# Two transformer blocks in one program: when the MLP writes the second block's split weight slabs to DRAM

## The chip, the cores and the metric

One core of a Trainium2 chip runs the whole program. Its engines are TensorE (PE, with its weight loads PEld), VectorE (DVE), ScalarE (ACT), GpSimd (POOL) and SyncE (SP), which issues nearly all DMAs. The metric is the device time of one execution in microseconds (us).

## The reference

The input `x` is 512 tokens by 1024 channels, float32. Two blocks follow each other:

```
# first block
h = rmsnorm(x, ln1);  z = h @ w_in
mix = [pooling means, chunked gated linear attention (decay, state), forgetting attention]
x = x + mix @ w_o
h = rmsnorm(x, ln2);  gate, up = split(h @ w_gu);  x = x + (silu(gate) * up) @ w_down   # MLP, 2816 wide
x = rmsnorm(x, ln_f)
# second block
h = rmsnorm(x, g);  q_lat, c_kv, k_rope, z_a, q_b, k_b, v_b, z_b, q_idx, k_idx, w_idx, gate_a, gate_b = split(h @ w_in)
y_a = latent attention(q_lat, c_kv, k_rope) * silu(z_a)
y_b = attention over the 128 keys chosen by the indexer (q_idx, k_idx, w_idx), plus a bias by distance, * silu(z_b)
merged = sigmoid(gate_a) * (y_a @ w_o_a) + sigmoid(gate_b) * (y_b @ w_o_b)
out = rmsnorm(x + merged @ w_out)
```

## The kernel before

**Products.** Channels lie on the partitions, tokens on the free axis. Every large product is made of float32 numbers split in two: a high part (`hi`, rounded by ACT's copy into the type fp32r) and a low part (`lo = src - hi`). One product of 128 by 128 by 512 is three matmuls, hi·hi, hi·lo, lo·hi (`dense`, L200). A weight slab (128 x 1024, 512 KB) is loaded into `wr`, ACT writes `wh`, and DVE or POOL writes `wl` (`weight`, L194; `split`, L186). There are two buffers of `wr` and three each of `wh` and `wl`.

**Order of the work.** TensorE's instructions run in the order in which the code writes them. The order on ACT, DVE, POOL and SP is chosen by the framework's scheduler when the program is built, from dependences, priorities and its own estimate of durations. Each of these engines then runs its list strictly in order and waits at the first instruction that is not ready. `issue_after(x)` orders the instructions of its block that run on the engine of `x` behind `x`; `high_priority` lets them go first.

**The first norm** (`block1`, L496): the squares of `x` are added on DVE into `ss`; PE sums them over channels (`tr<-ones,ss`), DVE makes `part` from the result, and PE spreads it over all partitions (`tr<-identr,part`), which ACT copies as `R`. The decay product of the gated linear attention (`tr<-ga,c_wau`, in `decay`) waits for `R`; the transposes `tr<-c_ident,b` need what is computed from it.

**The MLP** (`mlp`, L854) runs in two halves. A half has 11 gate/up iterations (two slabs of `w1gu` each, 48 matmuls), whose last step splits the result into `fh` (ACT) and `fl` (DVE); then eight down products (`down`, 33 matmuls each). A down product's weight of 704 KB is loaded into `wd` and split into `wdh` (ACT) and `wdl` (DVE); each of these has two buffers. Before the first iteration `entry` (L833) multiplies three slabs ahead of the second norm and spreads that norm's factor as `R`.

**Slabs split ahead.** During the MLP the kernel also prepares 27 slabs of the second block (`store`, L241): load into `sr` (two buffers), split into `sh` (ACT) and `sl` (POOL), one buffer each, and write both to DRAM (`h_w2s<-sh`, `l_w2s<-sl`, and the like for `w2pair`, `w2uq_r`). The second block then reads the two parts straight into `wh` and `wl` (`ready`, L231). The queue `ahead` (L884) holds these slabs; one is taken at the start of every gate/up iteration but the first, and one behind every second down product. Nothing but the buffers ties a `store` to that place.

**The bias by distance** (`relative`, L979, at the start of the second block): two small products make a table of 8 x 640 (`gd` in DRAM), and one DMA inside DRAM copies it 128 times per head into `shear` (2560 KB), from which each head of the last attention reads a skewed window.

Of the kernel before, what the change touches and what calls it, by code (L numbers as in the profile page):

```python
# [11 lines left out]
F32 = mybir.dt.float32  # L12
# [3 lines left out]
AF = mybir.ActivationFunctionType  # L16
# [68 lines left out]
class Body:  # L85
# [100 lines left out]
    def split(self, hi, lo, src, eng=None):  # L186

        self.nc.scalar.activation(hi, src, AF.Copy)  # L188
        (eng or self.nc.vector).tensor_tensor(lo, src, hi.bitcast(F32), op=OP.subtract)  # L189
# [37 lines left out]

    def slab(self, name, i, n=1024):
        return lambda: self.ready(name, i, n)
# [11 lines left out]
    def store(self, pool, name, i, n=1024):  # L241

        nc = self.nc
        raw = pool.tile([P, 1024], F32, tag="sr", name="sr", bufs=2)[:, :n]
        nc.sync.dma_start(raw, self.A[name][i])
        hi, lo = (pool.tile([P, 1024], F32R, tag=t, name=t, bufs=1)[:, :n] for t in ("sh", "sl"))
        self.split(hi, lo, raw, nc.gpsimd)
        self.stored[name, i] = kept = []
        for part, src in (("h", hi), ("l", lo)):
            kept.append(self.dp.tile([P, n], F32, name=f"{part}_{name}_{i}"))  # L250
            nc.sync.dma_start(kept[-1], src.bitcast(F32))
# [35 lines left out]
    def parts(self, c):  # L287

        n = c.shape[1]
        hi, lo = (self.gp.tile([P, 8], F32R, tag="part", name="part", bufs=6)[:, :n] for _ in "hl")  # L290
        self.nc.vector.tensor_copy(hi, c)
        self.nc.vector.tensor_tensor(lo, c, hi.bitcast(F32), op=OP.subtract)
        return hi, lo

    def spread(self, parts):

        ps = self.bank("tr")
        for t in range(NT):
            for a, c in enumerate(parts):
                self.mm(ps[:, t * P:(t + 1) * P], c[:, t:t + 1].to_broadcast([P, P]), self.identr, a == 0, a == 1)  # L300
        r = self.row()
        self.nc.scalar.activation(r, ps, AF.Copy)
        return r
# [9 lines left out]
    def square_into(self, ssum, src, first, scale=1.0, eng=None):  # L313
        nc = self.nc
        if first:
            nc.scalar.activation(ssum, src, AF.Square, scale=scale)
        else:
            sq = self.tmp()
            nc.scalar.activation(sq, src, AF.Square, scale=scale)  # L319
            (eng or nc.gpsimd).tensor_tensor(ssum, ssum, sq, op=OP.add)  # L320
# [175 lines left out]
    def block1(self, ctx, raw):  # L496
# [25 lines left out]
        for k in range(KD):  # L522
            with self.tc.issue_after(getattr(last, "ins", last)):
                self.square_into(ssum, x[k], k == 0, eng=nc.vector)
# [18 lines left out]
        next(gen)  # L543
        next(gen)
        R, Rc = self.all(r)
        psk = self.all(gen)
# [27 lines left out]
    def gla_phase(self, ctx, h, R, Rc, mix, mp, b, fd, psg, held, V, proj):  # L574
# [24 lines left out]
        def gates():  # L599
# [3 lines left out]
            nc.vector.tensor_tensor(z, psg[:64], t, op=OP.add)  # L603
# [9 lines left out]
        def gla_v():  # L613
            yield from self.take()
            w = [self.weight(A["w1gv"][a]) for a in range(2)]
# [7 lines left out]
        def qk(f, held=None):  # L623
            q, k = gx(), gx()
            ps = held[0] if held else (yield from self.dense(self.slab("w1s", T1["gq"] + f), h))
# [113 lines left out]
        def chain(f, held=None):  # L739
# [3 lines left out]
            yield QKW  # L743
# [109 lines left out]

    def mlp(self, ctx):  # L854
# [17 lines left out]
        def turn(m):  # L872
# [5 lines left out]
            for t in range(NT):  # L878
# [5 lines left out]
        t2 = lambda name, n: [("w2s", T2[name] + i, 1024) for i in range(n)]  # L884
        ahead = deque([("w2m", 0, KD * 72)] + t2("c_kv", 2) + t2("q_idx", 2) + t2("q_lat", 3) + [("w2kv_v", 0, 1024)]
                      + t2("gate_b", 8) + [("w2uq_r", 0, 768), ("w2pair", 0, 640)] + t2("gate_a", 2) + t2("z_a", 1)
                      + [("w2pair", 1, 640)] + t2("gate_a", 4)[2:] + t2("z_a", 2)[1:] + [("w2pair", 2, 640)])
        turns = []
        for half in range(2):
            for k in range(FH):  # L890
                m = half * FH + k
                if m and ahead:
                    self.store(wd, *ahead.popleft())
# [11 lines left out]
                self.split(act[k][0], act[k][1], u)  # L905
            for m in range(KD):
                ps = self.all(self.dense(down(m, half), act, kt=FH))
                if m % 2 and ahead:
                    self.store(wd, *ahead.popleft())
                nc.vector.tensor_tensor(x[m], ps, x[m], op=OP.add)  # L910
# [39 lines left out]
    def block2(self, ctx, psm, psc):  # L950
# [11 lines left out]
        relb = self.const(bp, "relb", [32, 8])  # L962
        wc = bp.tile([P, NT, 8], F32, name="wc")
        shear = self.dp.tile([8, P * 641], F32, name="shear")
# [13 lines left out]

        def relative():  # L979

            onehot = at("ph", 2, (P, 1024))[:32, :640]
            nc.sync.dma_start(onehot, A["onehot"])
            gd = self.dp.tile([8, 640], F32, name="gd")
            g8 = at("pl", 2, (P, 1024))[:8, :640]
            yield 9000
            for c in range(0, 640, 320):
                ps = self.bank("tr")
                self.mm(ps[:8, :320], relb, onehot[:, c:c + 320])
                nc.scalar.activation(g8[:, c:c + 320], ps[:8, :320], AF.Copy, scale=-1.0)
            nc.sync.dma_start(gd, g8)  # L990

            dst = bass.AP(tensor=shear.tensor, offset=shear.offset, ap=[[P * 641, 8], [641, P], [1, 640]])
            nc.sync.dma_start(dst, bass.AP(tensor=gd.tensor, offset=gd.offset, ap=[[640, 8], [0, P], [1, 640]]))
# [214 lines left out]
        self.spawn(relative())  # L1208
# [300 lines left out]
```

## Time and profile before

| | |
|---|---|
| median of 3 runs | 1075.25 us (1071.88 to 1076.89) |
| the profiled execution | 1080.48 us, of which the span from the first to the last instruction is 1078.7 us |
| PE busy | 1049.3 us, 97% of the span, 5264 matmuls |
| DVE, ACT, POOL busy | 654.2, 544.8, 368.5 us (61%, 51%, 34%) |
| mean granted clock of TensorE | 0.989 |
| DMA | 167.68 MB; slices 10 to 16 of 40 carry 257 to 355 GB/s, most others 57 to 230 |

The profile is one execution. A row of a timeline gives an instruction's start, its length, and in brackets the idle time of its engine just before it and what ended that idle time. A row of a window gives the busy time of each engine in a stretch, with the number of instructions, then TensorE's granted clock (1.00 is 2.4 GHz, 0.50 is 1.2 GHz), the share of time in which the DMA engines were busy, and GB/s. The matmul's length in the profile includes its pipeline; the pace is seen from starts.

### The profile page before, as it was taken

The numbers are of one execution on the slowest core, as the hardware profiler recorded it, in microseconds if no ns is written. First come the engines' busy times: TensorE is split into PE (matmuls) and PEld (weight loads), VectorE is DVE, ScalarE is ACT, GpSimd is POOL, SyncE is SP. The second block draws the span as 40 slices with busy tenths as digits, with TensorE's granted clock in tenths as the row PEclk, the third lists the DMA queues.
The fourth block names the chain that finished last, engine by engine and source line by source line (L and its number), as shares of the span: only waits on it lengthen the run. The fifth ranks groups of instructions, "written<-read, shape, count | busy, mean of one in ns | idle before, by whom it ended". The sixth has DMA issues, their size and how long they took to land.

```text
span 1078.7 us, 14278 instructions
## 1 busy us (share of the span) xinstructions
PE 1049.3 (97%) x5264; PEld 867.9 (80%) x5264; DVE 654.2 (61%) x1140; ACT 544.8 (51%) x954; POOL 368.5 (34%) x214
## 2 busy tenths in 40 slices
PE   8999999999999998999999999999999999999997
PEld 5888877787888776888888887888887898888786
DVE  6653488876656432345433335699995566887652
ACT  6763578746443432233314545545565556777233
POOL 2233322144555533223212310010024336655354
PEclk9999999999999998999999999999999999999999
DMA  6312222129898879432343146464532323335742
GB/s 224 104 59 79 62 104 64 67 80 355 288 320 302 287 257 310 163 111 83 107 141 100 57 147 226 165 216 163 177 125 81 117 78 118 110 99 166 282 145 79
DMA packets 57246, 167.68 MB, mean 155 GB/s; under 512 B 6680, under 2 KB 11176, under 8 KB 57176
## 3 DMA queue, kind: packets, MB, share of 16 engines
q1 hardware_dynamic: 54088, 160.45, 44.3%
q10 hardware_dynamic: 2448, 4.22, 1.0%
q0 software_dynamic: 640, 2.10, 0.5%
q8 instruction: 42, 0.69, 0.3%
q14 instruction: 28, 0.23, 0.1%
HBM read 129.81 MB, written 39.56 MB: 157 GB/s over the span
## 4 chain that ended last, share of the span: by engine, by line
PE 70%; DMA 12%; DVE 10%; ACT 4%; POOL 2%; issue 1%; SPq 1%; ACTq 0%; POOLq 0%; DVEq 0%
PE mm L151 57%; DMA h_w2s<-sh 6%; PE sc L151 5%; PE pv L151 3%; PE tr L158 2%; PE tr L151 2%; DMA l_w2s<-sl 2%; DMA wl<-l_w2s 1%; POOL sl L189 1%; ACT sh L188 1%; DMA h_w2pair<-sh 1%; DVE pl L409 1%; DVE b L333 1%; DVE score L1046 1%; DVE b L396 1%
## 5 line engine op out<-in xcount | busy, mean ns | idle before, releaser
L151 PE MATMUL mm<-hh,wh 128*128 128x512 f32 (+2 forms) x808 | 324.9, 402 | 4.8 <-ACT hh L516 1.9
L151 PE MATMUL mm<-hl,wh 128*128 128x512 f32 (+3 forms) x808 | 316.4, 392 | 0.6 <-DVE hl L517 0.6
L151 PE MATMUL mm<-hh,wl 128*128 128x512 f32 (+1 forms) x800 | 313.3, 392 | 1.1 <-DMA wl<-l_w2s 0.6
L189 POOL TENSOR_TENSOR wl<-wr,wh 128x1024 fp32r<-128x1024 f32 x80 | 198.9, 2487 | 332.5 <-ACT wh L188 311.2
L188 ACT ACTIVATE wh<-wr 128x1024 fp32r<-128x1024 f32 (+2 forms) x115 | 119.6, 1041 | 137.2 <-PE mm L151 107.0
L151 PEld LDWEIGHTS mm<-hh,wh 128*128 128x128 f32 (+1 forms) x808 | 153.1, 189 | 36.5 <-ACT hh L516 2.7
L151 PEld LDWEIGHTS mm<-hh,wl 128*128 128x128 f32 (+1 forms) x800 | 150.7, 188 | 34.7 <-DMA wl<-l_w2s 0.9
L151 PEld LDWEIGHTS mm<-hl,wh 128*128 128x128 f32 (+2 forms) x808 | 152.6, 189 | 29.0 <-DVE hl L517 1.9
L189 POOL TENSOR_TENSOR sl<-sr,sh 128x1024 fp32r<-128x1024 f32 (+3 forms) x27 | 66.6, 2466 | 77.3 <-DMA l_w2s<-sl 48.1
L151 PE MATMUL mm<-fh,wdh 128*128 128x512 f32 x176 | 71.8, 408 | 5.8 <-ACT fh L188 3.7
L151 PE MATMUL mm<-fh,wdl 128*128 128x512 f32 x176 | 71.5, 406 | 1.0 <-DVE wdl L189 0.9
L188 ACT ACTIVATE sh<-sr 128x1024 fp32r<-128x1024 f32 (+3 forms) x27 | 27.0, 1000 | 88.7 <-DMA h_w2s<-sh 46.0
L151 PE MATMUL mm<-fl,wdh 128*128 128x512 f32 x176 | 71.2, 404 | 0.4 <-DVE fl L189 0.4
L189 DVE TENSOR_TENSOR wl<-wr,wh 128x1024 fp32r<-128x1024 f32 (+1 forms) x34 | 51.7, 1522 | 25.4 <-ACT wh L188 24.1
L320 POOL TENSOR_TENSOR ss<-ss,t 128x512 f32<-128x512 f32 x21 | 30.2, 1446 | 101.1 <-ACT t L319 90.0
L189 DVE TENSOR_TENSOR fl<-u,fh 128x512 fp32r<-128x512 f32 x22 | 39.9, 1813 | 28.3 <-ACT fh L188 28.3
L409 DVE TENSOR_TENSOR pl<-tr,ph 128x128 fp32r<-128x128 f32 (+1 forms) x96 | 46.0, 483 | 11.2 <-ACT ph L408 10.1
L393 ACT ACTIVATE s<-s,m 128x128 f32<-128x128 f32 (+1 forms) x64 | 35.8, 560 | 31.8 <-DVE m L391 31.6
L151 PE MATMUL mm<-wh,hh 128*128 128x256 f32 x160 | 46.5, 290 | 0.0
L151 PEld LDWEIGHTS mm<-fh,wdh 128*128 128x128 f32 x176 | 34.1, 194 | 14.5 <-ACT fh L188 4.2
L910 DVE TENSOR_TENSOR x<-mm,x 128x512 f32<-128x512 f32 x16 | 11.0, 690 | 57.0 <-PE mm L151 57.0
L408 ACT ACTIVATE ph<-tr 128x128 fp32r<-128x128 f32 (+1 forms) x96 | 40.4, 426 | 9.9 <-PE tr L158 9.4
(343 smaller groups left out, 2038.8 us busy)
## 6 DMA issues: line engine op xcount, KB each, us to landing
wr<-in_w1gu SPq DMA_DIRECT2D x44, 512.0 KB, 4.4
wd<-in_w1d SPq DMA_DIRECT2D x16, 704.0 KB, 4.9
sr<-in_w2s SPq DMA_DIRECT2D x21, 512.0 KB, 5.6
h_w2s<-sh SPq DMA_DIRECT2D x21, 512.0 KB, 6.5
l_w2s<-sl SPq DMA_DIRECT2D x21, 512.0 KB, 3.9
wh<-h_w2s SPq DMA_DIRECT2D x21, 512.0 KB, 3.7
wl<-l_w2s SPq DMA_DIRECT2D x21, 512.0 KB, 4.6
wr<-in_w2s SPq DMA_DIRECT2D x18, 512.0 KB, 3.5
```

What stands on the lines that cost most here:

```text
L151: self.nc.tensor.matmul(out, l, r, start=start, stop=stop)
L158: self.nc.tensor.transpose(out, src, self.ident if ident is None else ident)
L188: self.nc.scalar.activation(hi, src, AF.Copy)
L189: (eng or self.nc.vector).tensor_tensor(lo, src, hi.bitcast(F32), op=OP.subtract)
L320: (eng or nc.gpsimd).tensor_tensor(ssum, ssum, sq, op=OP.add)
L333: nc.vector.tensor_tensor(q[x:x + 64], qf[o:o + 64], q[o:o + 64].bitcast(F32), op=OP.subtract)
L393: nc.scalar.activation(s[:, :n], s[:, :n], AF.Exp, scale=-1.0, bias=m[:, 0:1], accum_out=m[:, 1:2])
L396: nc.vector.tensor_scalar(s[:, :n], s[:, :n], m[:, 2:3], None, op0=OP.mult)
L408: nc.scalar.activation(hi, trv, AF.Copy)
L409: nc.vector.tensor_tensor(lo, trv, hi.bitcast(F32), op=OP.subtract)
L910: nc.vector.tensor_tensor(x[m], ps, x[m], op=OP.add)
L1046: nc.vector.match_replace(s, m8, s, -3.4e38)
```

## The change

1. `store` now takes its split behind the last split that the code wrote before it (`last_split`), and the call moves from the start of a gate/up iteration to its end. In the first half's down stage every product takes a store, not every second one.
2. Five more slabs are split ahead (`z_a` 2 and 3, `gate_a` 4 and 5, the fourth `w2pair`): 32 in all.
3. `relative` moves from the start of the second block into the first half's down stage: its two products stand behind the second down product.
4. In the first block the squares' adds get priority on DVE. The spread `tr<-identr,part` stands behind the third product, not ahead of its last three matmuls; the two slabs of `gv` are split on DVE, ordered behind the adds and behind `part`. The first slab of the second chain is ordered behind the spread's copy, and the decay product stands some 30 matmuls later.

```diff
     def split(self, hi, lo, src, eng=None):
-        self.nc.scalar.activation(hi, src, AF.Copy)
+        last = self.nc.scalar.activation(hi, src, AF.Copy)
+        self.last_split = getattr(last, "ins", last)
...
+    def first_slab(self, name, i):
+        with self.tc.issue_after(self.behind):
+            return self.weight(self.A[name][i])
...
         hi, lo = (pool.tile([P, 1024], F32R, tag=t, name=t, bufs=1)[:, :n] for t in ("sh", "sl"))
-        self.split(hi, lo, raw, nc.gpsimd)
+        with self.tc.issue_after(self.last_split):
+            self.split(hi, lo, raw, nc.gpsimd)
...
         for k in range(KD):
-            with self.tc.issue_after(getattr(last, "ins", last)):
-                self.square_into(ssum, x[k], k == 0, eng=nc.vector)
+            with self.tc.high_priority(), self.tc.issue_after(getattr(last, "ins", last)):
+                add = self.square_into(ssum, x[k], k == 0, eng=nc.vector)
+        self.added = getattr(add, "ins", add)
...
         next(r)
-        next(gen)
-        next(gen)
+        psk = self.all(gen)
         R, Rc = self.all(r)
-        psk = self.all(gen)
+        self.behind = self.spreaded
...
-            nc.vector.tensor_tensor(z, psg[:64], t, op=OP.add)
+            with self.tc.issue_after(self.parted):
+                nc.vector.tensor_tensor(z, psg[:64], t, op=OP.add)
...
-            w = [self.weight(A["w1gv"][a]) for a in range(2)]
+            w = []
+            for a, first in enumerate((self.added, self.parted)):
+                with self.tc.issue_after(first):
+                    w.append(self.weight(A["w1gv"][a], pool=False))
...
-            yield QKW
+            yield QKW + 3000 * (held is not None)
...
+    def relative(self, pool):
+        nc = self.nc
+        relb = self.const(pool, "relb", [32, 8])
+        onehot = self.const(pool, "onehot", [32, 640])
+        shear = self.shear = self.dp.tile([8, P * 641], F32, name="shear")
+        gd = self.dp.tile([8, 640], F32, name="gd")
+        g8 = pool.tile([8, 640], F32, name="g8")
+        yield
+        for c in range(0, 640, 320):
+            ps = self.bank("tr")
+            self.mm(ps[:8, :320], relb, onehot[:, c:c + 320])
+            nc.scalar.activation(g8[:, c:c + 320], ps[:8, :320], AF.Copy, scale=-1.0)
+        nc.sync.dma_start(gd, g8)
+        dst = bass.AP(tensor=shear.tensor, offset=shear.offset, ap=[[P * 641, 8], [641, P], [1, 640]])
+        nc.sync.dma_start(dst, bass.AP(tensor=gd.tensor, offset=gd.offset, ap=[[640, 8], [0, P], [1, 640]]))
+        yield
...
-        t2 = lambda name, n: [("w2s", T2[name] + i, 1024) for i in range(n)]
-        ahead = deque([("w2m", 0, KD * 72)] + t2("c_kv", 2) + t2("q_idx", 2) + t2("q_lat", 3) + [("w2kv_v", 0, 1024)]
-                      + t2("gate_b", 8) + [("w2uq_r", 0, 768), ("w2pair", 0, 640)] + t2("gate_a", 2) + t2("z_a", 1)
-                      + [("w2pair", 1, 640)] + t2("gate_a", 4)[2:] + t2("z_a", 2)[1:] + [("w2pair", 2, 640)])
+        t2 = lambda name, a, b: [("w2s", T2[name] + i, 1024) for i in range(a, b)]
+        ahead = [("w2m", 0, KD * 72)] + t2("c_kv", 0, 2) + t2("q_idx", 0, 2) + t2("q_lat", 0, 3) + [("w2kv_v", 0, 1024)]
+        ahead += t2("gate_b", 0, 8) + [("w2uq_r", 0, 768), ("w2pair", 0, 640)]
+        for p in range(4):
+            ahead += t2("gate_a", 2 * p, 2 * p + 2 if p < 3 else 6) + t2("z_a", p, p + 1)
+            ahead += [("w2pair", p + 1, 640)] if p < 3 else []
+        ahead = deque(ahead)
+        relative = self.relative(wd)
...
-                if m and ahead:
-                    self.store(wd, *ahead.popleft())
                 if m == 0:
                     self.entry()
...
                 self.split(act[k][0], act[k][1], u)
+                if m and ahead:
+                    self.store(wd, *ahead.popleft())
             for m in range(KD):
                 ps = self.all(self.dense(down(m, half), act, kt=FH))
-                if m % 2 and ahead:
+                if (m % 2 or half == 0) and ahead:
                     self.store(wd, *ahead.popleft())
+                if half == 0 and m < 2:
+                    next(relative)
...
-        self.spawn(relative())
```

The scheduler's order around the change, at three places. In these rows the left name is what an instruction writes.

ACT, end of the first half's gate/up and start of its down stage, before (`fh` is the last iteration's result, `sh` a store's high part, `wdh` a down weight):

```order
L900 ACTIVATE g<-g 128x512
L188 ACTIVATE sh<-sr 128x768
L188 ACTIVATE wh<-wr 128x1024
L188 ACTIVATE sh<-sr 128x640
L188 ACTIVATE fh_2558<-u 128x512
L188 ACTIVATE sh<-sr 128x1024
L188 ACTIVATE wdh<-wd 128x1408
```

and with the change:

```order
L935 ACTIVATE g<-g 128x512
L188 ACTIVATE wh<-wr 128x1024
L188 ACTIVATE fh_2558<-u 128x512
L188 ACTIVATE sh<-sr 128x1024 x2
L188 ACTIVATE wdh<-wd 128x1408
L188 ACTIVATE sh<-sr 128x1024
L188 ACTIVATE wdh<-wd 128x1408
```

Both stores that stood ahead of `fh` are gone from there; two now stand behind it, and then one ahead of each `wdh`.

SP, first half's down stage, with the change (`wd` are the down weights, `h_` and `l_` the parts that are written out); the `shear` DMA was in the second block before:

```order
L258 DMA h_w2s_3560<-sh 128x1024
L881 DMA gd<-g_3512 8x640
L900 DMA wd<-in_w1d 128x1408
L258 DMA l_w2s_3562<-sl 128x1024
L884 DMA shear<-gd 1024x1x640
L251 DMA sr<-in_w2s 128x1024
L258 DMA h_w2s_3619<-sh 128x1024
L258 DMA l_w2s_3621<-sl 128x1024
L251 DMA sr<-in_w2s 128x1024
L900 DMA wd<-in_w1d 128x1408 x2
L258 DMA h_w2s_3670<-sh 128x1024
```

and the place in the second block that it left, before:

```order
L238 DMA wl<-l_w2s_3224 128x1024
L990 DMA gd<-pl 8x640
L993 DMA shear<-gd 1024x1x640
L238 DMA wh<-h_w2s_2982 128x1024
L238 DMA wl<-l_w2s_2984 128x1024
```

Ahead of the `shear` DMA now stands the load of the sixth `wd` slab, and four transfers behind it the seventh; the indexer's slab `h_w2s_2982` no longer stands behind it.

ACT, entry of the last attention, before (`kst` and `qst` are operands of an attention head, `s` its scores, `wh` a weight slab):

```order
L188 ACTIVATE qst<-qf 64x512
L188 ACTIVATE qst<-qk 32x512
L188 ACTIVATE wh<-wr 128x1024
L393 ACTIVATE s,m<-s,m 128x512
L188 ACTIVATE qk<-kf 64x512
```

and with the change:

```order
L188 ACTIVATE qst<-qf 64x512
L188 ACTIVATE qst<-qk 32x512
L402 ACTIVATE s,m<-s,m 128x512
L188 ACTIVATE qk<-kf 64x512
L407 ACTIVATE s<-s,m 128x512
```

The slab between `qst` and `s,m` is one of the five that now come from DRAM already split, so ACT's half and POOL's half of its split are gone from here.

## Rows read from the trace of the kernel before

**Rows 1.** Windows of the MLP's first half and second half: busy us (x count), clock, DMA.
```profile
243.00:425.00 182.00, 172.66 (x750) 139.54 (x749) 94.16 (x77) 74.92 (x85) 91.73 (x37) 0.99 0.87 301
425.00:634.00 209.00, 209.00 (x924) 170.32 (x924) 84.11 (x84) 70.49 (x93) 50.35 (x26) 0.99 0.34 113
```
**Rows 2.** Windows around the five stalls: PE, PEld, DVE, ACT, POOL, clock, DMA, GB/s.
```profile
258.00:266.00 8.00, 6.40 (x33) 5.10 (x32) 4.22 (x6) 6.21 (x7) 3.95 (x2) 1.00 1.02 414
375.00:383.00 8.00, 3.90 (x11) 2.44 (x10) 1.72 (x2) 1.26 (x2) 5.66 (x3) 0.79 0.96 328
420.00:432.00 12.00, 8.97 (x27) 6.50 (x26) 3.85 (x3) 4.64 (x4) 3.34 (x2) 0.72 0.96 339
672.00:680.00 8.00, 6.27 (x24) 5.45 (x23) 5.28 (x8) 2.39 (x4) 1.28 (x1) 0.79 0.63 226
812.00:820.00 8.00, 5.33 (x21) 4.28 (x20) 6.42 (x11) 3.17 (x6) 5.21 (x4) 0.79 0.21 66
```
**Rows 3.** Timeline of ACT at the first stall.
```profile
261.40 1.06 ACT L188 ACTIVATE sh<-sr 128x1024 fp32r<-128x1024 f32 x1 [0.67 <-DMA h_w2s<-sh]
262.37 0.58 ACT L302 ACTIVATE R<-tr 128x512 f32<-128x512 f32 x1
```
**Rows 4.** Timeline of ACT in the first half's down stage.
```profile
377.93 0.74 ACT L188 ACTIVATE sh<-sr 128x640 fp32r<-128x640 f32 x1 [3.63 <-DMA h_w2uq_r<-sh]
378.57 0.61 ACT L188 ACTIVATE fh<-u 128x512 fp32r<-128x512 f32 x1
...
415.32 1.06 ACT L188 ACTIVATE sh<-sr 128x1024 fp32r<-128x1024 f32 x1 [5.65 <-DMA h_w2pair<-sh]
420.76 1.06 ACT L188 ACTIVATE sh<-sr 128x1024 fp32r<-128x1024 f32 x1 [4.38 <-DMA h_w2s<-sh]
421.72 1.36 ACT L188 ACTIVATE wdh<-wd 128x1408 fp32r<-128x1408 f32 x1
```
**Rows 5.** Timeline of SP: the `shear` DMA is issued.
```profile
655.91 0.77 SPq L993 DMA_DIRECT2D shear<-gd  x1
```
**Rows 6.** Chain of waits at the fourth stall: start, us, what.
```profile
661.41 14.10 DMA wl<-l_w2s
```
**Rows 7.** Timeline of DVE at the fifth stall.
```profile
807.48 0.68 DVE L189 TENSOR_TENSOR kst<-qf,qst 64x512 fp32r<-64x512 f32 x1
...
810.46 2.51 DVE L189 TENSOR_TENSOR kst<-qf,qst 64x512 fp32r<-64x512 f32 x1
813.00 1.66 DVE L189 TENSOR_TENSOR kst<-qk,qst 32x512 fp32r<-32x512 f32 x1
```
**Rows 8.** Timeline of POOL and of ACT at the fifth stall.
```profile
810.02 2.40 POOL L189 TENSOR_TENSOR wl<-wr,wh 128x1024 fp32r<-128x1024 f32 x1 [3.08 <-ACT wh L188]
812.38 1.73 POOL L189 TENSOR_TENSOR qk<-kf,qk 64x512 fp32r<-64x512 f32 x1
...
815.58 0.72 ACT L398 ACTIVATE s<-s,m 128x512 f32<-128x512 f32 x1 [4.42 <-DVE m L394]
```
**Rows 9.** Chain of waits: one down product at full pace.
```profile
578.15 7.70 PE mm L151 x33
```
**Rows 10.** DMA issues: what, KB each, median us from issue to landing.
```profile
h_w2s<-sh SPq DMA_DIRECT2D x21, 512.0 KB, 6.5
...
shear<-gd SPq DMA_DIRECT2D x1, 2560.0 KB
```
**Rows 11.** Timeline of DVE: the low half of a down weight.
```profile
401.74 1.62 DVE L189 TENSOR_TENSOR wdl<-wd,wdh 128x1408 fp32r<-128x1408 f32 x1 [3.08 <-ACT wdh L188]
```
**Rows 12.** Costliest groups: POOL's half of a store (busy, mean ns, idle before).
```profile
L189 POOL TENSOR_TENSOR sl<-sr,sh 128x1024 fp32r<-128x1024 f32 (+3 forms) x27 | 66.6, 2466 | 77.3 <-DMA l_w2s<-sl 48.1
```
**Rows 13.** Timelines of DVE, ACT and PE in the first block.
```profile
39.78 0.69 DVE L653 TENSOR_TENSOR b<-gx,b 128x512 f32<-128x512 f32 x1
...
32.62 1.28 ACT L455 ACT_TABLE_LOAD   x1
...
43.52 0.60 PE L158 MATMUL tr<-c_ident,b 128*128 128x128 f32 x4
```

More of the change, by code (lines that the diff above doesn't have):

```diff
@@ L291, in parts @@
         self.nc.vector.tensor_copy(hi, c)
-        self.nc.vector.tensor_tensor(lo, c, hi.bitcast(F32), op=OP.subtract)
+        last = self.nc.vector.tensor_tensor(lo, c, hi.bitcast(F32), op=OP.subtract)
+        self.parted = getattr(last, "ins", last)
         return hi, lo
@@ L301, in spread @@
         r = self.row()
-        self.nc.scalar.activation(r, ps, AF.Copy)
+        last = self.nc.scalar.activation(r, ps, AF.Copy)
+        self.spreaded = getattr(last, "ins", last)
         return r
@@ L319, in square_into @@
             nc.scalar.activation(sq, src, AF.Square, scale=scale)
-            (eng or nc.gpsimd).tensor_tensor(ssum, ssum, sq, op=OP.add)
+            return (eng or nc.gpsimd).tensor_tensor(ssum, ssum, sq, op=OP.add)
     def acts(self):
@@ L624, in qk @@
             q, k = gx(), gx()
-            ps = held[0] if held else (yield from self.dense(self.slab("w1s", T1["gq"] + f), h))
+            first = () if held else self.first_slab("w1s", T1["gq"] + f)
+            ps = held[0] if held else (yield from self.dense(lambda: first, h))
             nc.vector.scalar_tensor_tensor(q, ps, 0.125, R, op0=OP.mult, op1=OP.mult)
@@ L961, in block2 @@
         klo = self.half_zero(bp)
-        relb = self.const(bp, "relb", [32, 8])
         wc = bp.tile([P, NT, 8], F32, name="wc")
-        shear = self.dp.tile([8, P * 641], F32, name="shear")
+        shear = self.shear
         score = {i: bp.tile([P, (i + 1) * P], F32, name=f"score{i}") for i in range(1, NT)}
@@ L977, in block2 @@
         nc.vector.tensor_tensor(KI[64:96], kidx, KI[0:32].bitcast(F32), op=OP.subtract)
[L979 to L993, printed above, removed]
         def index_scores(j):
```

## The prediction

> **What bounds the kernel now.** I began with the page: PE is busy for 97% of the span, so time can be lost only where PE waits or where its clock is halved. The waits by engine then name what PE waited for, and windows show where. The second half of the MLP has no idle PE at all; the first half, with almost the same code, has 182.0 - 172.66 = 9.3 us of it [rows 1]. The difference between the halves is on the DMA side: 301 GB/s against 113, since nearly all 27 stores run in the first half. The places are few [rows 2]. The method for each is the same: the window's length less PE's busy time is idle; the length times (1 - granted clock) is what the lower level (1.2 of 2.4 GHz) behind it costs.
>
> - 258 to 266: idle 1.6, clock full. Together 1.6.
> - 375 to 383: idle 4.1, clock 0.21 x 8 = 1.7. Together 5.8.
> - 420 to 432: idle 3.0, clock 0.28 x 12 = 3.4. Together 6.4.
> - 672 to 680: idle 1.7, clock 1.7. Together 3.4.
> - 812 to 820: idle 2.7, clock 1.7. Together 4.4.
>
> The first three have one cause, and it is on ACT's list, not on PE's. A store's `sh` has one buffer, so ACT waits until the previous `h_` write has landed, and all behind it waits too: `R` behind the `sh` at 261.40 [rows 3]; `fh` behind the one at 377.93, after 3.63 us of waiting for `h_w2uq_r`; `wdh` behind two of them at 415.32 and 420.76, which waited 5.65 and 4.38 us [rows 4]. The fourth is a load: the `shear` copy is issued at 655.91 [rows 5], and the `wl` load issued 5.5 us behind it takes 14.10 us to land [rows 6]. The fifth is DVE's: a `kst` that takes 0.68 us alone takes 2.51, then another 1.66 [rows 7], while POOL splits a slab (810.02 to 812.42) and then writes `qk` [rows 8]; ACT's `s` comes 4.42 us late and PE's transposes with it.
>
> **The change, part by part.**
>
> *Pacing the stores.* In the new order no `sh` stands ahead of `R` or of `fh`, and a gate/up iteration has one store. 48 matmuls at 7.70 / 33 = 0.233 us [rows 9] make 11.2 us for it, and the chain of a store is 1.06 for `sh` [rows 4] plus 6.5 to the landing [rows 10], so the next `sh` finds its buffer free. I take all three stalls as gone: -13.8. The bounds are 0 (if each comes back elsewhere, rival C) and -13.8.
>
> *Stores in the down stage.* There each product has one store, 7.70 us against 1.06 + 6.5 = 7.6. This is tight, but a `wdh` may be up to 7.70 - 1.36 - 1.62 = 4.7 us late [rows 4, 11] before PE sees it. Without the `shear` copy I put it at 0.
>
> *`relative` moved.* Its two products cost PE the same at either place. Gone is the fourth stall, since the indexer's slab no longer stands behind the copy: -3.4 (bounds 0 and -3.4). But the copy now runs where DMA is busiest. Let T = 0 be the start of the first down product. ACT's `fh` is done near 2; then come `sh`, a landing, a second `sh`, a landing, a third: 2 + 2 x 7.6 = 17. Behind it stand a `wdh` and the copy of the table, then the write of `gd` and its landing, some 5 us together: `shear` goes out at T = 22 (estimate from rows 4 and 10). In the trace, the second 512 KB load behind it landed 661.41 + 14.10 - 655.91 = 19.6 us after the copy's issue [rows 5, 6]. In the new order the seventh `wd` slab is the fifth transfer behind it: `sr`, `h_`, `l_`, `sr`, then `wd`. Two more of 0.52 MB at 301 GB/s [rows 1] are 3.5 us, and 0.72 MB is 2.4: 25.5. Ahead of the copy stand a `wd` and an `l_` just issued, 1.24 MB or 4.1 us, of which I take 2.5 as still to come. The slab lands at 22 + 2.5 + 25.5 = 50.0, `wdh` is done at 51.4. PE wants it after six products and `relative`'s two, 6 x 7.70 + 1 = 47.2. So PE idles 4.2 us, about 1 more for `wdl`, which takes 1.62 [rows 11] while two matmuls run, and the clock costs what it cost behind the like stalls, 1.7 to 3.4 [rows 2]; I take 2.0, nearer to the single stall of 375. Sum **+7.2**; bounds 0 (all 4.2 us gained elsewhere, by an earlier copy or a nearly empty queue) and +12 (4 us later, and the longer drop of the clock).
>
> The Trainium skill (DMA: Bandwidth & Descriptors, Rules for kernel authors) says that an outermost dimension under 16 confines a DMA to that many of the 16 engines; the copy's destination begins with 8 heads. The trace agrees: of the 19.6 us two loads take 3.5, which leaves 16.1 for 2.62 MB [rows 10], 163 GB/s against 301. Spread over all engines it would take 8.7, the slab would land at 42.6, and the sum would be that of rival B.
>
> *Five more slabs split ahead.* In the second half they add 5 x 1.06 on ACT, which is busy 70 of 209 us, and 5 x 2.47 on POOL [rows 12], busy 50 of 209 [rows 1], and 2.6 MB in and 5.2 out where DMA carries 113 GB/s: 0, hidden by 209 us of PE that never waits; if that cover goes, it is rival D. In the second block they take away POOL's split at 810.02, beside which the first `kst` took 2.51 in place of 0.68, that is 1.8 us of the 2.7 that PE idled. The second `kst` stays beside POOL's `qk`. I take half of the fifth stall: **-2.2** (bounds 0 and -4.4).
>
> The Trainium skill (SBUF — State Buffer, Who interferes with whom) says that a DVE instruction with two SBUF inputs and a POOL instruction hold a shared pair of ports one at a time. The trace agrees, both `kst` end 0.55 us behind POOL's instruction; by that rule alone the second `kst` keeps its 1.66, which is why half and not the whole fits.
>
> *The first block.* PE's matmuls are the same in another order. The slack is between the product for the decay's end, 39.78 + 0.69, and the transposes at 43.52, 3.0 us [rows 13]. ACT's list gets two more table loads of 1.28 in that chain; the decay product moves back by about 3 us and the transposes by 15 matmuls, 3.4 us, so 3.0 + 3.4 - 3 - 2.6 = 0.8 us of slack stays. I take 0; bounds 0 (PE had nothing to gain there) and +3.
>
> **Sum.** 1080.5 - 13.8 - 3.4 - 2.2 + 7.2 = 1068.3 for a profiled execution. The profiled execution of before was 1080.48 where the median of the runs is 1075.25; by the same ratio the runs should give **1063**.
>
> **Rivals.** Half a per cent, 5.4 us, is about what a measurement of this kernel can tell from no change: faster is below 1069.9, slower above 1080.6.
>
> - *B, the copy stays hidden.* The same without +7.2: 1061.1, or 1056. For it speaks that 4.2 us hang on an estimate of T = 22 and of the queue; against it that the landing is measured and four transfers stand between.
> - *C, the jam only moves.* The down stage had some eight stores before and has eight now, seven of full size, and the copy besides. If landings take longer than 6.5 there, `sh` again holds up `wdh`, and the 12.2 us of the second and third stall come back: 1080.5 - 1.6 - 3.4 - 2.2 + 7.2 = 1080.5, or 1075. For it speaks that 7.6 is so near to 7.70; against it that only the place with two `sh` in a row stalled on `wdh` before [rows 4].
> - *D, slower: loads held up on SP's list.* SP runs in order, and every iteration of both halves now has `h_`, `l_` and `sr` between two loads of `w1gu`. A slab is loaded four slabs ahead, 4 x 24 x 0.233 = 22 us. From the end of an iteration `sh` 1.06, `sl` and a `wl` ahead of it 2 x 2.47, landing 6.5, `wh` 1.06 and `wl` 2.4 make 16. It decides once landings pass 12.5 us, as the 14.10 did [rows 6]. Then some 20 iterations lose as much as the first stall, 1.6 each: 1063 + 32 = 1095. Against it: 5 transfers of 0.52 MB in 11.2 us are 234 GB/s, under the 301 that the first half carried.
>
> **How the numbers follow.** The forecast has 0.49 (its own range 1058 to 1071), B 0.28, C 0.17, D 0.06. Faster: 0.46 of the forecast, B, and 0.01 of C, 0.75. Same: 0.03 of the forecast and 0.14 of C, 0.17. Slower: D and 0.02 of C, 0.08. The range 1052 to 1073 takes in B with the fifth stall gone as a whole (1054), the forecast with the dearer `shear` stall, and leaves out most of C and D.
>
> **What would show it.** Right: ACT's `R` and `fh` wait for PE or DVE, never behind an `sh`; the gate/up windows of both halves show PE busy throughout and about 230 GB/s; one idle stretch of PE, released by ACT's `wdh`, some 45 us into the first down stage, behind a `wd` that took over 15 us to land; no wait for `wl` at the indexer; `kst` at 0.68. Wrong: several stalls on `wdh` in the down stage (C), PE waiting for DMA or `wh` in the gate/up (D), the stall at the last attention unchanged, or a new wait of PE at the decay's transposes in the first block.

## The result and the profile after

The changed kernel took **1063.99 us** (median of 4 runs, 1063.20 to 1064.61) against 1075.75 us for the kernel before, run beside it (4 runs, 1071.88 to 1076.89). The ratio is 0.9897, with a 95% interval of 0.987 to 0.9923. So it is faster by about one per cent, where 1063 was forecast in a range of 1052 to 1073. The profiled execution of the change is 1063.43 us with a span of 1061.7, among its other runs. That of before, 1080.48, is slower than all 41 runs of that kernel timed in this study (1069.43 to 1079.71). Both matter below. One later execution of the change took 2082.58 us, with every matmul at half its pace, and has no part in any number below.

The windows of the changed kernel come first: the two halves of the MLP [rows 1], then the places of the five old stalls [rows 2] as far as they can be found again, with the new one at 414 us.

```profile
243.00:425.00 182.00, 179.46 (x782) 145.61 (x781) 83.77 (x78) 69.47 (x79) 74.07 (x29) 0.99 0.74 252
425.00:617.00 192.00, 192.00 (x853) 157.59 (x852) 83.19 (x78) 77.91 (x100) 84.24 (x40) 1.00 0.65 221
258.00:266.00 8.00, 8.00 (x39) 6.45 (x38) 4.36 (x9) 6.46 (x8) 2.40 (x1) 1.00 0.54 183
375.00:383.00 8.00, 8.00 (x35) 5.50 (x34) 2.33 (x3) 2.83 (x4) 3.22 (x1) 1.00 0.98 321
656.00:664.00 8.00, 8.00 (x37) 6.56 (x36) 5.86 (x10) 3.69 (x7) 1.34 (x1) 1.00 0.38 131
795.00:803.00 8.00, 8.00 (x40) 6.51 (x39) 7.11 (x16) 5.28 (x10) 3.11 (x3) 1.00 0.45 161
414.00:422.00 8.00, 5.50 (x16) 4.07 (x17) 4.74 (x3) 3.70 (x3) 2.37 (x1) 0.79 0.87 301
```

The old stalls are gone: in the four places that can be found again PE had been busy for 3.90 to 6.40 of 8 us and is now busy for 8.00. The third, on `wdh`, has no such place; the new stall, also on `wdh`, stands in the same stage. DMA traffic is spread over both halves, 252 and 221 GB/s where it was 301 and 113. The new stall, of 2.5 us, stands at 414, with the clock at 0.79. The waits of PE (who waits, for what; total us, times, longest us) name it, and two more that were not forecast, on `b` and on `part`:

```profile
PE sc L151 <- ACT b L693: 1.8, 1, 1.8
...
PE mm L151 <- ACT wdh L188: 1.6, 1, 1.6
...
PE tr L151 <- DVE part L298: 1.1, 2, 0.9
PE mm L151 <- DVE wdl L190: 0.9, 1, 0.9
...
PE tr L151 <- DVE part L299: 0.5, 1, 0.5
```

**The stall on `wdh`.** SP's queue, then ACT:

```profile
387.58 0.77 SPq L884 DMA_DIRECT2D shear<-gd  x1
388.40 6.83 SPq L251 DMA_DIRECT2D sr<-in_w2s  x1
...
397.83 1.09 SPq L900 DMA_DIRECT2D wd<-in_w1d  x1
```

```profile
409.95 1.06 ACT L188 ACTIVATE sh<-sr 128x1024 fp32r<-128x1024 f32 x1 [10.21 <-DMA h_w2s<-sh]
414.14 1.38 ACT L188 ACTIVATE wdh<-wd 128x1408 fp32r<-128x1408 f32 x1 [3.13 <-DMA wd<-in_w1d]
```

The `shear` copy goes out, the issue of the next load itself takes 6.83 us, and the `wd` slab issued at 397.83 lands at 414.0, 16.2 us later. The first down product starts at 366.22 in this trace. On the prediction's scale, where T = 0 is that start, the copy is thus issued at T = 21.4 (forecast 22) and the slab lands at T = 47.8 (forecast 50.0).

**The wait in the first block.** On ACT the copy of the transposes (`b<-tr`, the kernel's `kt`) now stands behind a slab's split, which waits for its load. PE's `sc<-gv` products wait for that copy:

```profile
46.27 1.06 ACT L188 ACTIVATE wh<-wr 128x1024 fp32r<-128x1024 f32 x1 [3.87 <-DMA wr<-in_w1s]
47.23 0.58 ACT L693 ACTIVATE b<-tr 128x512 f32<-128x512 f32 x1
```

Before, two splits were over at 43.3 and the copy ran at 44.16.

The lengths of the stages place everything else. Each is taken from the start of a stage's first matmul to that of the next one's, in us, in the profiled execution of each kernel (experiments below). The first `lat` product is the first `mm<-lat,wh`, the first `ya` product the first `mm<-ya,wh`; "second half" is that of the MLP:

| kernel | to the last `w_o` product | first gate/up | first down | second half | to the first `lat` product | to the first `ya` product | to the end |
|---|---|---|---|---|---|---|---|
| before | 243.56 | 124.79 | 73.86 | 183.95 | 69.37 | 221.38 | 161.79 |
| the change | 244.16 | 122.06 | 67.35 | 183.87 | 66.03 | 216.95 | 161.24 |
| first block undone | 243.49 | 122.06 | 70.04 | 183.88 | 67.64 | 216.93 | 164.76 |
| `relative` moved back | 241.35 | 122.10 | 61.36 | 183.94 | 69.74 | 216.86 | 161.52 |
| wide copy | 241.31 | 122.07 | 62.73 | 183.87 | 66.06 | 216.96 | 161.17 |
| 27 slabs | 243.32 | 122.07 | 65.32 | 183.85 | 66.06 | 221.49 | 161.42 |
| pacing alone | 243.71 | 122.09 | 61.36 | 183.84 | 67.53 | 219.75 | 161.74 |
| two `sh` buffers | 243.72 | 122.06 | 68.83 | 183.87 | 67.25 | 219.78 | 161.81 |
| wide copy, moved back | 244.38 | 122.06 | 61.36 | 183.85 | 66.15 | 216.99 | 161.40 |

From before to the change: +0.6, -2.7, -6.5, -0.1, -3.3, -4.4, -0.6, together -17.0 us.

One execution of a kernel differs from the next in these lengths, and the clock is a large part of it: behind the same wait of PE it falls to 1.2 GHz in one trace and stays at 2.4 in another. The fifth stall shows it, with 27 slabs in both: pacing alone, then "27 slabs":

```profile
796.00:806.00 10.00, 7.36 (x43) 6.07 (x42) 7.04 (x15) 5.22 (x12) 4.25 (x3) 1.00 0.31 106
798.00:808.00 10.00, 7.36 (x33) 5.82 (x32) 6.79 (x13) 3.88 (x9) 4.24 (x3) 0.83 0.29 106
```

PE is busy for 7.36 of 10 us in both, but does 43 matmuls in the one and 33 in the other, at a granted clock of 1.00 and 0.83; the stretches to the first `ya` product are 219.75 and 221.49. So a difference of under 2 us between two single traces need not be an edit's.

### The profile page after: what moved, and what is told of

Read it like the earlier page. It is cut to its first block, busy times and chain, and to the rows that moved or that the text cites. A ratio compares the mean times of both kernels' runs of the same rounds, so it can differ in the third digit from the quotient of the medians.

```text
span 1061.7 us, 14307 instructions
## 1 busy us (share of the span) xinstructions
PE 1042.3 (98%) x5264; PEld 864.3 (81%) x5264; DVE 644.2 (61%) x1141; ACT 548.3 (52%) x956; POOL 371.1 (35%) x213
## 4 chain that ended last, share of the span: by engine, by line
PE 47%; DVE 10%; DMA 3%; ACT 2%; issue 1%; SPq 1%; POOL 1%; ACTq 0%; DVEq 0%; POOLq 0%
PE mm L151 39%; PE sc L151 3%; DVE score L1068 2%; PE pv L151 2%; PE tr L158 2%; DVE m L1067 2%; DMA wd<-in_w1d 2%; PE tr L151 1%; DVE kst L190 1%; SPq L251 1%; DVE s L400 1%; DVE z L1203 1%; DMA z<-gate_a 1%; DVE pl L418 1%; DVE score L1052 1%
## 5 line engine op out<-in xcount | busy, mean ns | idle before, releaser
L190 POOL TENSOR_TENSOR wl<-wr,wh 128x1024 fp32r<-128x1024 f32 x74 | 186.6, 2522 | 328.6 <-ACT wh L188 307.2
L188 ACT ACTIVATE wh<-wr 128x1024 fp32r<-128x1024 f32 (+1 forms) x110 | 115.1, 1046 | 175.3 <-PE mm L151 150.1
L151 PEld LDWEIGHTS mm<-hl,wh 128*128 128x128 f32 (+2 forms) x808 | 151.8, 188 | 29.1 <-DVE hl L526 1.8
L190 POOL TENSOR_TENSOR sl<-sr,sh 128x1024 fp32r<-128x1024 f32 (+3 forms) x32 | 81.9, 2558 | 81.0 <-DMA l_w2s<-sl 52.0
L938 DVE TENSOR_TENSOR u<-mm,R 128x512 f32<-128x512 f32 x22 | 15.2, 691 | 67.2 <-PE mm L151 67.2
L418 DVE TENSOR_TENSOR pl<-tr,ph 128x128 fp32r<-128x128 f32 (+1 forms) x96 | 45.9, 483 | 13.2 <-ACT ph L417 12.2
L402 ACT ACTIVATE s<-s,m 128x128 f32<-128x128 f32 (+1 forms) x64 | 35.8, 560 | 32.0 <-DVE m L400 31.6
L190 DVE TENSOR_TENSOR fl<-u,fh 128x512 fp32r<-128x512 f32 x22 | 42.4, 1925 | 14.7 <-ACT fh L188 14.7
L188 ACT ACTIVATE sh<-sr 128x1024 fp32r<-128x1024 f32 (+3 forms) x32 | 31.7, 990 | 37.3 <-DMA h_w2s<-sh 30.2
L190 DVE TENSOR_TENSOR wl<-wr,wh 128x1024 fp32r<-128x1024 f32 (+1 forms) x35 | 42.9, 1226 | 11.0 <-ACT wh L188 10.6
L329 POOL TENSOR_TENSOR ss<-ss,t 128x512 f32<-128x512 f32 x21 | 29.7, 1423 | 55.3 <-ACT t L328 43.5
```

What stands on the lines that cost most here:

```text
L151: self.nc.tensor.matmul(out, l, r, start=start, stop=stop)
L188: last = self.nc.scalar.activation(hi, src, AF.Copy)
L329: return (eng or nc.gpsimd).tensor_tensor(ssum, ssum, sq, op=OP.add)
L402: nc.scalar.activation(s[:, :n], s[:, :n], AF.Exp, scale=-1.0, bias=m[:, 0:1], accum_out=m[:, 1:2])
L418: nc.vector.tensor_tensor(lo, trv, hi.bitcast(F32), op=OP.subtract)
L938: nc.vector.tensor_tensor(u, ps, self.R2, op=OP.mult)
```

## The experiments

Two theories stood against each other. One: the pacing of the stores is the gain, and the move of the `shear` copy gives its own gain back as a stall on `wdh`. The other: the denser stores themselves make `wdh` late, and the gain needs the parts together.

**Pacing alone.** The kernel before with this alone (27 slabs, `relative` and the first block as before):

```diff
+        with self.tc.issue_after(self.last_split):
             self.split(hi, lo, raw, nc.gpsimd)
...
-                if m and ahead:
-                    self.store(wd, *ahead.popleft())
...
                 self.split(act[k][0], act[k][1], u)
+                if m and ahead:
+                    self.store(wd, *ahead.popleft())
...
-                if m % 2 and ahead:
+                if (m % 2 or half == 0) and ahead:
```

> The kernel before with the pacing of the stores alone: each store behind its iteration's last split, one after each product of the first down stage; 27 slabs, relative and the first block as before. Theory: the pacing is what the change is worth, three stalls of the first half, 2.7 in the gate/up and 12.5 in the first down stage, while the other edits nearly cancel (shear stall +4.9 on wdh for -3.4 at the indexer, fifth stall -4.4, first block about -1): 15 us under a before of 1076 to 1079, that is 1061 to 1064, about the time of the whole change, and the first down stage takes 61.4 us. Rival: the pacing needs relative or the 32 slabs beside it; then the down stage keeps over 65 us and the time is over 1066.

Measured: 1061.89 us (1060.44 to 1064.56, 6 runs), ratio 0.9882 (0.9857 to 0.9906). Its windows of the first down stage and the first gate/up:

```profile
365.80:427.20 61.40, 61.40 (x265) 49.49 (x264) 24.24 (x17) 19.92 (x18) 22.97 (x10) 1.00 0.85 295
243.70:365.80 122.10, 122.10 (x547) 101.05 (x546) 63.54 (x62) 52.21 (x62) 55.52 (x21) 1.00 0.68 235
```

PE never waits there. The pacing alone is worth 12.5 + 2.7 = 15.2 us in the traces and gives the whole gain: in the runs it stands 2 us under the change, which is within what one measurement can tell apart. The one edit both puts each store behind what PE waits for and spreads the stores over both halves; these two were not tried apart.

**A second buffer for `sh`.** The kernel before, with `bufs=2` for `sh` in place of 1:

```diff
-pool.tile([P, 1024], F32R, tag=t, name=t, bufs=1)
+pool.tile([P, 1024], F32R, tag=t, name=t, bufs=2 if t == "sh" else 1)
```

> The kernel before with a second buffer for sh and nothing else. Theory: the stalls of the first half are ACT waiting in sh for the h_ write that still reads its one buffer; with two buffers most of these waits go, and with them most of the 15 us without any pacing: 1061 to 1067. Rival: it is the flood of transfers itself, or sl's one buffer and POOL, that makes wdh late; then the first down stage keeps over 70 us and the time stays within 4 us of 1076.

Measured: 1069.13 us (1067.11 to 1072.32, 10 runs), ratio 0.9948 (0.9929 to 0.9967): faster, but above the 1061 to 1067 that were expected. The first stall is gone, and those at 415 and 421, as the theory says. One stall stays, at the start of the down stage, and ACT's timeline shows why:

```profile
374.01 0.74 ACT L188 ACTIVATE sh<-sr 128x640 fp32r<-128x640 f32 x1 [5.91 <-DMA sr<-in_w2pair]
...
375.60 0.61 ACT L188 ACTIVATE fh<-u 128x512 fp32r<-128x512 f32 x1
```

The `sh` ahead of `fh` no longer waits for its buffer but for its own input, whose load stands in the flood (324 GB/s over the first gate/up, where the pacing has 235). So the one buffer was half of the cause (7.8 of the 15.2 us in the traces), and the other half is an `sh` that stands ahead of `fh` and waits for a late load. The pacing takes both away.

**`relative` moved back** to the second block, the rest as in the change (the function, its constants and the `shear` tensor stand where they stood before):

```diff
-        relative = self.relative(wd)
...
-                if half == 0 and m < 2:
-                    next(relative)
...
+        self.spawn(relative())
```

> The changed kernel with relative (its constants, two products and the shear copy) back at the start of the second block. Theory: the stall on wdh at 414 us comes from the shear copy and goes, 2.5 us idle and 1.7 of clock, so the first down stage gains 4; the stall at the indexer, where wl stands behind the copy, comes back with 3.4. Together within 1 us of the change, 1063 to 1065, with the two places changed. Rival: the stall at 414 comes from the denser stores themselves; then it stays, the indexer's comes back, and the time is 1067 to 1068.

Measured: 1059.19 us (1058.64 to 1059.62, 4 runs), ratio 0.985 (0.9823 to 0.9876). That is under both expectations. The first down stage runs without a gap:

```profile
363.40:424.80 61.40, 61.40 (x264) 49.41 (x264) 22.10 (x17) 20.36 (x18) 25.63 (x10) 1.00 0.87 307
```

The stall on `wdh` is the copy's and not the stores': the stage is 6.0 us shorter, where 4 were expected; 1.4 of them are the two products. The indexer's stall came back (69.74 where the change has 66.03), and the first block, whose code is the same, was 2.8 us shorter in this trace, of which more below.

**The copy written another way**, 128 rows outermost in place of 8 heads, the same 1024 pieces:

```diff
-        dst = bass.AP(..., ap=[[P * 641, 8], [641, P], [1, 640]])
-        nc.sync.dma_start(dst, bass.AP(..., ap=[[640, 8], [0, P], [1, 640]]))
+        dst = bass.AP(..., ap=[[641, P], [P * 641, 8], [1, 640]])
+        nc.sync.dma_start(dst, bass.AP(..., ap=[[0, P], [640, 8], [1, 640]]))
```

> The changed kernel with the shear copy's dimensions written in another order, 128 rows outermost in place of 8 heads; the same 1024 pieces of 2560 bytes. Theory: the copy then runs on all 16 DMA engines, takes about half as long, the wd slab behind it lands within 9 us in place of 16.2, and the stall on wdh at 414 us goes: 4 us faster, 1060. Rival: the copy is bound by its 1024 pieces whatever the order; then the landing stays near 16 us and the time at 1064.

Measured: 1057.53 us (1056.02 to 1060.45, 5 runs), ratio 0.9848 (0.9819 to 0.9876). The DMA share (second last column) in the 4 us in which the copy runs by itself, first in the change, then with the wide copy:

```profile
390.00:394.00 4.00, 4.00 (x19) 3.23 (x18) 2.62 (x2) 1.38 (x1) 2.41 (x1) 1.00 0.50 185
```

```profile
390.00:394.00 4.00, 4.00 (x19) 3.23 (x18) 2.47 (x1) 0.00 (x0) 0.99 (x1) 1.00 1.05 248
```

With the narrow copy the engines were busy for half of the time. The Trainium skill's rule (DMA: Bandwidth & Descriptors, Rules for kernel authors), that an outermost dimension under 16 leaves the other engines without work, agrees with the 0.50. The rate rises by 248 / 185 = 1.34 and not by 2, so "half as long" in the expectation was too much. It suffices: the slab behind the copy lands in time. SP's queue, then ACT, with the wide copy:

```profile
384.56 0.66 SPq L884 DMA_DIRECT2D shear<-gd  x1
385.26 1.06 SPq L251 DMA_DIRECT2D sr<-in_w2s  x1
...
392.50 6.41 SPq L900 DMA_DIRECT2D wd<-in_w1d  x2
```

```profile
406.91 1.38 ACT L188 ACTIVATE wdh<-wd 128x1408 fp32r<-128x1408 f32 x1 [3.11 <-DMA wd<-in_w1d]
```

That is T = 43.5, where PE wants it at 47.2, and the down stage takes 62.73. The expectation had the slab land within 9 us of its issue; it took 14.3. More than half of the 4.3 us gained is the earlier issue: the `sr` issue behind the copy takes 1.06 us in place of 6.83, and the `wd` load goes out at T = 29.1 in place of 31.6.

**The change and the wide copy again**, beside each other on another chip:

> The changed kernel once more, unaltered, beside the next two on the same chip. Theory: 1064 again, with a stall on wdh in the first down stage (67 us or more where the pacing alone took 61.4) whose size differs from run to run by some 2 us. Rival: the 6.5 us by which the wide copy was faster belong to the chip it ran on; then this kernel takes under 1060 here.

> The wide copy once more, beside the change on the same chip. Theory: 5 to 7 us faster than the change, 1057 to 1059, of which 4 to 5 are in the first down stage (62.7 us) and up to 2.8 in the first block, where its landing is a matter of the run. Rival: under 3 us faster, if the gain was in the first block alone.

Measured: the wide copy again 1057.53 us (1057.13 to 1059.18, 5 runs; ratio 0.9841, 0.9811 to 0.987), with 62.74 us in the first down stage. The change: ratio 0.9896 (0.9857 to 0.9934), its five comparable runs between 1058.99 and 1069.90 with 1062.38 in the middle. So the wide copy gains about 5 us on this chip too. The change's five spread over 11 us and the wide copy's over 2. The stall on `wdh` differs between traces (2.6 to 7.3 us, below); that it makes the spread of these runs, none of which was traced, is not shown.

**The wide copy with `relative` back** in the second block (the last two edits together):

> The wide copy with relative back at the start of the second block, so the copy runs where the MLP's stores are over. Theory: the first down stage takes 61.4 us and the indexer's wait for its slab behind the copy, 3.6 us with the narrow copy, shrinks to 0 to 2, since the copy is over sooner: 1055 to 1058, as fast as the wide copy in the MLP or a little faster, so moving relative was not needed. Rival: the indexer still waits 3 us or more; then 1058 to 1060.

Measured: 1058.03 us (1057.58 to 1059.54, 6 runs), ratio 0.9846 (0.9817 to 0.9875). The down stage takes 61.36 and the stretch to the first `lat` product 66.15, 0.1 longer than in the change. PE has no wait for `wl`, and at the old stall it is busy:

```profile
656.00:664.00 8.00, 8.00 (x41) 7.14 (x41) 7.24 (x11) 2.99 (x5) 1.77 (x2) 1.00 0.80 302
```

Once the copy is wide, it may stand at either place; the move was not needed.

**27 slabs**: the change without the five more (`gate_a` 4 and 5, `z_a` 2 and 3, the fourth `w2pair`):

```diff
-        for p in range(4):
-            ahead += t2("gate_a", 2 * p, 2 * p + 2 if p < 3 else 6) + t2("z_a", p, p + 1)
-            ahead += [("w2pair", p + 1, 640)] if p < 3 else []
+        ahead += t2("gate_a", 0, 2) + t2("z_a", 0, 1)
+        ahead += [("w2pair", 1, 640)] + t2("gate_a", 2, 4) + t2("z_a", 1, 2) + [("w2pair", 2, 640)]
```

> The changed kernel with 27 stored slabs in place of 32. Theory: the stall of the last attention stage near 800 us, 4.4 us with its clock, was DVE's kst beside POOL's split of a slab and comes back, since POOL splits gate_a and z_a there again: 4 us slower, 1068. Rival: that stall went for another reason (the whole program stands 16 us earlier there, other neighbours); then the time stays within 1 us of 1064.

Measured: 1065.78 us (1061.92 to 1067.90, 6 runs), ratio 0.9911 (0.9886 to 0.9936). That is under the 1068 expected, and in the runs no clear difference from 1064; in the trace the stretch to the first `ya` product takes 221.49 where the change has 216.95. DVE and POOL with 27 slabs:

```profile
795.49 2.50 DVE L190 TENSOR_TENSOR kst<-qf,qst 64x512 fp32r<-64x512 f32 x1
798.03 1.66 DVE L190 TENSOR_TENSOR kst<-qk,qst 32x512 fp32r<-32x512 f32 x1
```

```profile
795.05 2.40 POOL L190 TENSOR_TENSOR wl<-wr,wh 128x1024 fp32r<-128x1024 f32 x1 [3.07 <-ACT wh L188]
797.41 1.73 POOL L190 TENSOR_TENSOR qk<-kf,qk 64x512 fp32r<-64x512 f32 x1
```

And in the change:

```profile
798.40 0.68 DVE L190 TENSOR_TENSOR kst<-qf,qst 64x512 fp32r<-64x512 f32 x1
799.11 0.68 DVE L190 TENSOR_TENSOR kst<-qk,qst 32x512 fp32r<-32x512 f32 x1
```

```profile
799.11 1.83 POOL L190 TENSOR_TENSOR qk<-kf,qk 64x512 fp32r<-64x512 f32 x1 [21.69 <-ACT qk L188]
```

Without POOL's split the first `kst` is not held up, so the second starts together with POOL's `qk` instead of behind its start, and takes 0.68 too. All four traces with 27 slabs have a 2.50 or 2.51 and a 1.65 or 1.66 here, and all eight with 32 have 0.68 or 0.69 twice. The order of the starts shows at another place in the change too: a `kst` at 697.24, 0.03 us ahead of a POOL instruction, takes 0.69, and the next one at 698.03, while that instruction still runs, 1.59. Of the 4.5 us, 1.7 are the clock's: pacing alone and two `sh` buffers have the same slow `kst`, no drop of the clock behind them, and 219.75 and 219.78.

**The first block undone**: the change with the next norm's adds, the spread, the `gla_v` slabs and the decay product as before.

```diff
-            with self.tc.high_priority(), self.tc.issue_after(...):
+            with self.tc.issue_after(...):
...
-        psk = self.all(gen)
-        R, Rc = self.all(r)
-        self.behind = self.spreaded
+        next(gen)
+        next(gen)
+        R, Rc = self.all(r)
+        psk = self.all(gen)
...
-            yield QKW + 3000 * (held is not None)
+            yield QKW
```

> The changed kernel with its edits of the first block taken back (the order of the adds and of the spread, the gla_v slabs, the decay product's place); stores, relative and the 27 + 5 slabs as in the change. Theory: the edits of the first block cost what the trace of the change shows in the product for sc at 45.6, 2.4 us by which that landmark came later; then this kernel is 2 to 4 us faster than the change, 1060 to 1062, and has no wait of PE's sc<-gv products on ACT. Rival: the edits pay back in the gated linear attention behind them what they cost there; then it is within 1 us of 1064 and the landmark at the last w_o product stands where it stood, or it is slower by up to 3.

Measured: 1065.22 us (1064.03 to 1070.58, 6 runs), ratio 0.9914 (0.9888 to 0.994): not the 2 to 4 us faster that were expected, but the rival. (Its profiled execution, 1070.58, the slowest of the six, holds a wait of 2.7 us on `lat` at 995 us that no other trace has.) The same taken back from the wide copy's kernel:

> The wide copy's kernel with the edits of the first block taken back. This measures those edits without the stall on wdh beside them. Theory: they gain 2.2 us where the slab that wh waits for lands in time (transposes' block 129.35 against 131.54 us at the first causal product) and lose 0.6 where it lands late; so this kernel is 1 to 2 us slower than the wide copy and its times lie closer together, 1058.5 to 1060. Rival: the edits gain nothing; then it is as fast as the wide copy or faster, 1057 or less.

Measured: 1059.15 us (1057.09 to 1062.81, 6 runs), ratio 0.9856 (0.9832 to 0.988). In both pairs the undone block is slower by 1.2 to 1.6 us, less than the runs differ, and the times of the second do not lie closer together, as its theory had it. The traces say more: the first `causal` product starts at 131.14 to 131.76 us in the five traces with the old block, and at 129.35, 129.35, 130.95, 131.37, 132.19 and 132.39 in six with the new one. So the edits gain up to 2.2 us or lose up to 0.8. PE's wait for `b` goes with it: 0.3 us in the two at 129.35, 1.5 and 1.9 in the next two, 1.8 and 1.7 in the last two, where the clock fell behind it too. They gain nothing that these timings could show.

**The `kt` copy ahead of the splits**, on top of the wide copy:

```diff
+            self.copied = getattr(copied, "ins", copied) if f == 0 else None
...
+        with self.tc.issue_after(after) if after is not None else ExitStack():
             self.split(hi[:, :n], lo[:, :n], raw[:, :n], ...)
```

> The wide copy's kernel with one more edit: on ACT the copy of the transposes (kt) goes ahead of the two slab splits that stand before it, so that it no longer waits for a slab's landing. Theory: the stall of PE's sc<-gv at 46 to 48 us, 0.7 in the good runs and 2.3 with a half clock behind it in the others, goes in all runs; so the times lie closer together, at 1055.5 to 1056.5, where the wide copy's lay at 1056 to 1060.5. Rival: the slabs split later make PE wait elsewhere in the gated linear attention; then the time stays at 1057 to 1060 or rises.

Measured: 1059.24 us (1057.75 to 1060.58, 5 runs), ratio 0.9852 (0.9829 to 0.9875): the rival's time. The wait on `b` is gone, and another has come:

```profile
PE pv L151 <- DVE at L725: 1.8, 2, 1.0
```

## Why the prediction was right, and where not

The time and most places were right; two errors of opposite sign cancel in the number, so that 1063 came so near to 1063.99 is in part luck.

- **Pacing, -13.8.** Right in place and cause: -15.2. The gate/up gave 2.7 in place of 1.6, since PE lost another 0.6 and 0.3 us at 357 and 363 (by the starts of its matmuls), outside the windows that were read. The margin was not where the prediction had it, though. `sh` still waits for `h_` (10.21 us at 409.95); that is in the time of the copy, and the `wdh` behind it then waits 3.13 us more for its own load. In the trace with `relative` moved back `sh` waits up to 4.39 us for `h_`, and the `wdh` behind it still has to wait for PE. Rival C had no part: the stage takes 61.36 with eight stores and no copy.
- **The `shear` stall, +7.2.** Right in kind, place and cause. Against the wide copy's 62.73, where the same products run and `wdh` is on time, it is 4.6 us in the change's trace, 7.3 with the first block undone and 2.6 with 27 slabs. What failed is that the step gave one number where a landing decides: T = 47.8 in the change, 50.4 in the trace with 7.3, for 50.0 in the forecast. PE waited 2.5 us in the change, 4.5 and 2.0 in the other two, for 5.2 in the forecast; behind the 2.0 the clock did not fall. Rival B is the wide copy's kernel: T = 43.5 (42.6 forecast), and 1057.5 us (1056 forecast).
- **"Its two products cost PE the same at either place"** was wrong by 1.4 us. In the first down stage they are added in full (62.73 with the wide copy, 61.36 without them). In the second block they had filled waits of PE for the norm's `part`, 1.1 and 0.5 us in the change and 0.7 with the wide copy moved back, so the stretch to `lat` is 66.15 with them and 66.06 without.
- **The indexer, -3.4:** -3.3, with some luck in the pair of traces. The cause is right: with the narrow copy in the second block PE waits 0.6 to 2.1 us for `wh` and `wl` in all four traces, with the copy moved in none. But the stretch takes 69.37 and 69.74 where the clock fell in it and 67.53 and 67.25 where it did not, and 67.64 in the trace with the first block undone, where it fell with the copy moved. So the move is worth 1.2 to 3.7 us here by the traces.
- **The fifth stall, -2.2:** -4.4, the bound, of which 1.7 are a drop of the clock that two of four traces with 27 slabs do not have; without it the gain is 2.8. The step that failed is "the second `kst` stays beside POOL's `qk`": how long it takes hangs on which of the two starts first, and with the first `kst` on time it is DVE.
- **Five slabs in the second half, 0:** 183.87 with them, 183.85 without. Rival D had no part.
- **The first block, 0:** +0.6 here, -2.2 to +0.8 by trace. The slack was worked out on the chain of the decay; what ended it was a slab's split ahead of the copy on ACT, which no step had looked at. PE's wait for that copy, 1.8 us, comes right behind the transposes, where the prediction had put one of its signs of being wrong.
- **"By the same ratio".** The terms gave -12.2 and the traces show -17.0. The 5 us by which before's profiled execution exceeded its median were scaled into the forecast as if the change kept them. The traces point to the fourth and fifth stall, which the change removes: these two stretches take 290.75 us in before and 287.28 and 287.03 with pacing alone and with two `sh` buffers, whose code there is that of before, and there the clock did not fall. That is 3.5 to 3.7 of the 5 us; with one trace of before it is not shown. The change's profiled execution is near its own median. Without that step, and with the terms as they were, the forecast would have been 1068.

## A version that beats both

The change with the wide copy: 1057.53 us, measured twice on two chips, 5 to 6.5 us under the change and 17 to 19 under the kernel before. With `relative` in the second block again it is 1058.03, the same within the runs' spread; so the copy's place is free.

## What to carry to other kernels

A helper's instruction that waits for a buffer or a load must not stand on an in-order engine ahead of one that the bottleneck waits for. Putting it behind, which here also spread the helpers out, gave all of the gain; a second buffer gave about half. When a long transfer is moved to hide it, look first whether it can be made shorter: with another order of its dimensions the copy did not have to be moved at all. A profiled execution that lies above its runs may hold more of the very stalls that are to go, so a sum made against it should not be scaled back by the same ratio. And when two traces are compared, look at the granted clock behind each wait before a difference of 1 to 2 us is given to an edit.

## What was not expected of the hardware

The wide copy's pieces of 2560 bytes each took longer: in the 4 us shown above, in which nothing else was moved, 112 ns on the mean of the trace's records for the narrow copy, 174 for the wide one. So 2.1 times the busy share (1.05 for 0.50) gave 1.34 times the rate. And the issue of a DMA on SP can itself take 6.83 us, at 388.40, right behind the copy, where it mostly takes 0.3 to 0.8. Everything later on SP's list stands behind it, the `wd` load at 397.83 among it. In the two other traces with the narrow copy in the MLP that issue takes 7.60 and 5.12 us, in the four with the wide copy there 0.64 to 1.06.
